# Sums of weight blocks made in DRAM by adding DMAs, in a two-layer trunk on one core

## The chip, the cores and the metric

The kernel runs on one core of a Trainium2 chip. The metric is the device time of one execution in microseconds (us); the median of three runs of the kernel before is 855.57 us, from 854.59 to 857.61. The engines of the core are TensorE (PE: matmuls, with PEld for its weight loads), VectorE (DVE), ScalarE (ACT), GpSimd (POOL) and SyncE (SP, which here only issues DMAs). Each works through its own instructions in order, and waits between engines go by semaphores.

## The reference

Two layers over 512 tokens of width 1024, each a norm, a mixer and a residual add, and a last norm. Cut to what matters:

```python
def pool_mixer(h, w_in, w_grp, scale, w_out):          # layer 0
    v, gate = jnp.split(h @ w_in, 2, axis=-1)          # 2 x 2048 columns
    p = multiscale_pool(v)                             # windows of 2, 4, 8, 16 tokens, by group of 512
    m = jnp.einsum('btgc,gcd->btgd', p, w_grp).reshape(B, T, D_INNER) * scale
    return (m * jax.nn.silu(gate)) @ w_out

def hgrn2_mixer(h, w_in, lb, norm_g, w_out):           # layer 1
    q, fz, i, gate = jnp.split(h @ w_in, 4, axis=-1)   # 4 x 2048 columns
    # forget gates f from fz, k from 1 - f; per head of 128 columns a recurrence over the tokens:
    #   S_t = diag(f_t) S_{t-1} + k_t v_t^T,   o_t = S_t^T q_t        with v = i
    # in chunks, with running products of f within a chunk
    ...
    return (o * jax.nn.silu(gate)) @ w_out

for layer in range(2):
    h = h + mixer(rms_norm(h, norm_g[layer]))          # rms_norm: h * rsqrt(mean(h*h) + eps) * g
return rms_norm(h, final_g)
```

All is in float32.

## The kernel before, in words

**Products.** A float32 product is three matmuls (`mm3`, L128): both operands are cut into a high part (a cast on ACT, L97) and a low part (a subtraction on DVE, L98). Weights come in pieces of 128 x 2 x 512 (512 KB): SP loads a piece into one of three buffers `wraw`, and `split` makes `whi` and `wlo`, six buffers each (`piece`, L100). The norm is not put into the operand: the products run on h times the norm's weights, and the norm's factor `rn`, one number for a token, is spread over the partitions by matmuls (`spread`, L192, its matmuls on L197) into `rb`, by which the results are multiplied.

**Layer 0** goes through four groups of 512 columns: values (L263), pooling on DVE (L274), gates with silu (L290; its last product is `gs` on POOL, L300), the group's product with `w_grp` (L304), and the product out (L220). The first products of group 0 don't need the factor. It is made from the squares of the tokens in the first microseconds: `ms` on DVE, then `rn_l0` on POOL (L255); the matmuls of L197 that spread it are written into the gates' first product ahead of its last two blocks (L258).

**Layer 1** goes through four groups of four heads. `prepare` (L692) makes the forget gates (`forget`, L396), their running products within a chunk by doubling steps on DVE (L698 to L702), the queries, and scales keys and queries (L713 to L723). For group 0 it also calls, by `mid`, `turn` (transposes of h) and `differences` (L433): sums and differences of the operand's four blocks (two halves of the tokens, two halves of the 1024 rows), cut in two and also stored in DRAM.

**The values of two groups at once.** `inputs2` (L464) makes the values of groups g and g + 1 for g = 0 and 2: with the operand as 2 x 2 blocks and the weights as 2 x 2 blocks of 512 x 512 (`row`: half of the inner dimension, `col`: group), seven block products do the work of eight. Four of them take a sum of weight blocks: b00 + b01, that + b11, b01 + b11, and b00 + b01 + b11 + b10. The kernel before loads the blocks and adds them on DVE (`add`, L483, traced as L485) before it cuts them (`cut`, L488), with running sums in the tile `chain`: eight adds of 128 x 1024 and 18 loads of 512 KB for a pair.

**The order.** The program is not run in the order in which it is written. A scheduler at build time goes through the instructions, engine by engine, by priority (as written, with loads and splits moved ahead by `tc.high_priority`), and puts on each engine what its own model says can go next. The result is a fixed order for each engine. No DMA is issued from POOL in the kernel before; SP issues the loads, ACT the stores.

Of the kernel before, what the change touches and what calls it, by code (L numbers as in the profile page):

```python
# [40 lines left out]
P = 128  # L41
D = 1024
T = 512
DI = 2048
# [11 lines left out]
AHEAD0 = 85  # L56
AHEAD = 300
FLOOR = 1e-26
LEVELS = (1, 2, 4, 8, 16, 32, 64)


# [5 lines left out]
def trunk(ctx: ExitStack, tc: tile.TileContext, xT, x_d, par, ident_d, causal_d, mask_d, fg_d, w0_in, w0_grp, w0_out, w1_in, w1_out, out):  # L67
# [28 lines left out]
    def split(src, hi, lo):  # L96
        nc.scalar.copy(out=hi, in_=src)  # L97
        nc.vector.tensor_tensor(out=lo, in0=src, in1=hi, op=ALU.subtract)  # L98
# [124 lines left out]
            nc.vector.tensor_tensor(out=h[n], in0=acc, in1=h[n], op=ALU.add)  # L223


    with tc.tile_pool(name="l0", bufs=1) as l0:
        xs, pieces = [], []
        wv = w0_in.rearrange("(k p) n -> p k n", p=P)
# [86 lines left out]
        zprev = None  # L315
        for g in range(NG):
            vs = values(g)
            px = pool(g, vs)
            if zprev is not None and g < NG - 1:
                project_out(load_out(w0_out, g - 1), zprev)  # L320
            gts = gates0(g)
            z = mixed(g, px, gts)
            if g == NG - 1:
                project_out(load_out(w0_out, g - 1), zprev)
            zprev = z
# [24 lines left out]
    def hgrn(ctx, general, h):  # L350
# [113 lines left out]
        def inputs2(g):  # L464

            w = w1_in.rearrange("(k p) n -> p k n", p=P)

            def block(row, col, i):
                c = 2 * DI + (g + col) * GC
                return w[:, 4 * row + 2 * i:4 * row + 2 * i + 2, c:c + GC]

            def load(*a):
                raw = wpool.tile([P, 2, GC], F32, name="wraw", tag="wraw", bufs=RAW)
                with tc.high_priority(AHEAD):
                    nc.sync.dma_start(out=raw, in_=block(*a))  # L480
                return raw

            def add(out, x, y):  # L483
                with tc.high_priority(AHEAD):
                    nc.vector.tensor_tensor(out=out, in0=x, in1=y, op=ALU.add)  # L485
                return out

            def cut(x):  # L488
                hi = wpool.tile([P, 2, GC], F32R, name="whi", tag="whi", bufs=WB)
                lo = wpool.tile([P, 2, GC], F32R, name="wlo", tag="wlo", bufs=WB)  # L490
                with tc.high_priority(AHEAD):
                    split(x, hi, lo)
                return [(hi[:, 0], lo[:, 0]), (hi[:, 1], lo[:, 1])]

            def product(accs, x, pieces):
                for b, acc in enumerate(accs):
                    t = slice(b * P, (b + 1) * P)
                    for k, ((xh, xl), (wh, wl)) in enumerate(zip(x, pieces)):
                        mm3(acc, xh[:, t], xl[:, t], wh, wl, k == 0, k == 3)

            two = lambda: [ps.tile([P, T], F32, name="mm", tag="mm", bufs=4) for _ in range(2)]
            v = l1.tile([P, TB, GC], F32, name="vn", tag="vn", bufs=1)
            v1 = [l1.tile([P, GC], F32, name="v1", tag="gs", bufs=4) for _ in range(TB)]
            chain = []
            s = (lambda i: diff[i]) if g == 0 else again

            def plus(out, acc, x):
                nc.vector.tensor_tensor(out=out, in0=acc, in1=x, op=ALU.add)

            def times(x, by, t):  # L510
                nc.scalar.activation(out=x, in_=x, func=AF.Copy, scale=by[:, t:t + 1])

            a = two()
            product(a, own[0], cut(load(0, 0, 0)) + cut(load(0, 0, 1)))
            for b in range(2):
                nc.scalar.copy(out=v[:, 2 + b], in_=a[b])
            a = two()
            product(a, own[1], cut(load(1, 0, 0)) + cut(load(1, 0, 1)))
            for b in range(2):
                plus(v[:, b], a[b], v[:, 2 + b])  # L520
                times(v[:, b], rn, b)
            pieces = []
            for i in range(2):
                x, y = load(0, 0, i), load(0, 1, i)
                chain.append(l1.tile([P, 2, GC], F32, name="chain", tag="f", bufs=2))
                pieces += cut(add(chain[i], x, y))
            c = two()
            product(c, s(0), pieces)
            s2 = s(1)
            pieces = [x for i in range(2) for x in cut(add(chain[i], chain[i], load(1, 1, i)))]  # L530
            a = two()
            product(a, s2, pieces)
            s3 = s(2)
            for b in range(2):
                plus(v1[b], a[b], v[:, 2 + b])
            pieces = []
            for i in range(2):
                x, y = load(0, 1, i), load(1, 1, i)
                pieces += cut(add(x, x, y))
            a = two()  # L540
            product(a, s3, pieces)
            s4 = s(3)
            for b in range(2):
                plus(v[:, 2 + b], a[b], v1[b])
                plus(v1[2 + b], c[b], v[:, 2 + b])
                plus(v1[b], c[b], v1[b])
                times(v1[2 + b], nrn, 2 + b)
                nc.scalar.dma_start(out=v_d[2 + b], in_=v1[2 + b])
            pieces = [x for i in range(2) for x in cut(add(chain[i], chain[i], load(1, 0, i)))]
            a = two()  # L550
            product(a, own[3], pieces)
            for b in range(2):
                plus(v[:, 2 + b], a[b], v[:, 2 + b])
                times(v[:, 2 + b], rn, 2 + b)
            a = two()
            product(a, s4, cut(load(1, 1, 0)) + cut(load(1, 1, 1)))
            for b in range(2):
                plus(v1[b], a[b], v1[b])
                times(v1[b], nrn, b)
                nc.scalar.dma_start(out=v_d[b], in_=v1[b])  # L560
            return v
# [108 lines left out]
        def factored():  # L670
# [21 lines left out]
            def prepare(g, mid=None):  # L692
                cur["first"] = firsts = [l1.tile([P, 2, TB], F32, name="first", tag="first", bufs=2) for _ in range(2)]
                es = []
                fs, ks = forget(g, store)
                for pr in range(2):
                    f, kk = fs[pr], ks[pr]
                    for hh in (1, 2, 4, 8, 16, 32):  # L698
                        x = f.rearrange("p j (b s m two h) -> p (j b) s m two h", b=TB, s=2, two=2, h=hh)
                        n = 32 // hh  # L700
                        nc.vector.tensor_tensor(out=x[:, :, 0, :, 0], in0=x[:, :, 0, :, 0], in1=x[:, :, 0, :, 1, 0:1].broadcast_to([P, 2 * TB, n, hh]), op=ALU.mult)
                        nc.vector.tensor_tensor(out=x[:, :, 1, :, 1], in0=x[:, :, 1, :, 1], in1=x[:, :, 1, :, 0, hh - 1:hh].broadcast_to([P, 2 * TB, n, hh]), op=ALU.mult)  # L702

                    en = ends[:, g * GT + 2 * pr:g * GT + 2 * pr + 2]
                    fv = f.rearrange("p j (b s c) -> p j b s c", b=TB, s=2)
                    nc.gpsimd.tensor_copy(out=en[:, :, :, 0], in_=fv[:, :, :, 0, 0])
                    nc.gpsimd.tensor_copy(out=en[:, :, :, 1], in_=fv[:, :, :, 1, 63])
                    e = l1.tile([P, 4, 2, TB], F32, name="e", tag="e", bufs=2)[:, 0]
                    nc.gpsimd.tensor_tensor(out=e, in0=firsts[pr], in1=en[:, :, :, 0], op=ALU.mult)
                    es.append(e)  # L710
                if mid:
                    mid()
                qs = queries(g)  # L713
                for pr in range(2):
                    for j in range(2):
                        r = l1.tile([P, T], F32, name="r", tag="r", bufs=2)
                        nc.gpsimd.tensor_scalar(out=r, in0=fs[pr][:, j], scalar1=FLOOR, scalar2=None, op0=ALU.max)  # L717
                        nc.vector.reciprocal(out=r, in_=r)  # L718
                        rv, fv, kv, qv = halved(r), halved(fs[pr][:, j]), halved(ks[pr][:, j]), halved(qs[pr][:, j])
                        nc.gpsimd.tensor_tensor(out=kv[:, :, 0], in0=kv[:, :, 0], in1=fv[:, :, 0], op=ALU.mult)  # L720
                        nc.gpsimd.tensor_tensor(out=kv[:, :, 1], in0=kv[:, :, 1], in1=rv[:, :, 1], op=ALU.mult)  # L721
                        nc.vector.tensor_tensor(out=qv[:, :, 0], in0=qv[:, :, 0], in1=rv[:, :, 0], op=ALU.mult)  # L722
                        nc.vector.tensor_tensor(out=qv[:, :, 1], in0=qv[:, :, 1], in1=fv[:, :, 1], op=ALU.mult)  # L723
                cur["k"], cur["q"], cur["e"] = ks, qs, es
# [242 lines left out]
```

## Time and profile before

| | |
|---|---|
| median of three runs | 855.57 us (854.59 to 857.61) |
| profiled execution | 856.04 us, span 854.2 us, mean granted clock 0.986 |
| PE busy | 818.0 us, 96% of the span |
| DVE busy | 606.8 us, 71% |
| ACT busy | 302.2 us, 35% |
| POOL busy | 153.9 us, 18% |
| DMA | 104.24 MB, mean 122 GB/s |

Layer 0 takes about the first 314 us, layer 1 the rest. "Busy" counts the instructions of an engine, not the issuing of DMAs. PEclk in the slices is the clock that TensorE was granted, in tenths of its full speed (9 is 0.9 or more); 0.5 of full speed is the lower of its two levels, 1.2 GHz against 2.4. "Idle before" an instruction is put down to what released it last.

### The profile page before, as it was taken

Reading aid. Unit: us, or ns where it says so; the run is one execution under the profiler, and the core shown is the slowest. Engines: PE = TensorE matmul, PEld = TensorE weight load, DVE = VectorE, ACT = ScalarE, POOL = GpSimd, SP = SyncE. Lnnn points to the kernel's source line nnn. Section 1 sums busy time; section 2 is a strip of 40 time slices with the busy share of each in tenths; the row PEclk is TensorE's granted clock in tenths of the full one; section 3 lists DMA queues with packets and bytes.
Section 4 is the critical chain, followed back from the end, with each engine's and each line's share of the span. In section 5 each row is a group of like instructions: output and inputs, shape, how many; then the busy total and the mean of one; then the engine's idle time right before and its main releaser. Section 6 shows DMA issues by size and latency. Waiting matters only on the chain.

```text
span 854.2 us, 10355 instructions
## 1 busy us (share of the span) xinstructions
PE 818.0 (96%) x3854; PEld 681.8 (80%) x3854; DVE 606.8 (71%) x917; ACT 302.2 (35%) x508; POOL 153.9 (18%) x198
## 2 busy tenths in 40 slices
PE   9999999999999999977899998999988999998995
PEld 8888888888888888856688887888867888887984
DVE  5687546835777464998856996569988645996764
ACT  7442223223234254433544313223135143313222
POOL 0020010001020050620022332103300021332200
PEclk9999999999999999987999999999999999999999
DMA  9532233322124353156764221223178343221202
GB/s 348 174 100 80 70 117 128 99 99 98 50 99 151 94 183 107 60 196 197 229 214 148 79 79 43 96 99 91 58 256 277 106 148 99 79 84 57 79 2 101
DMA packets 52172, 104.24 MB, mean 122 GB/s; under 512 B 3984, under 2 KB 8336, under 8 KB 52112
## 3 DMA queue, kind: packets, MB, share of 16 engines
q1 hardware_dynamic: 45056, 91.24, 32.7%
q10 hardware_dynamic: 7056, 12.25, 3.9%
q8 instruction: 32, 0.52, 0.3%
q14 instruction: 28, 0.23, 0.1%
HBM read 92.99 MB, written 10.49 MB: 121 GB/s over the span
## 4 chain that ended last, share of the span: by engine, by line
PE 78%; DVE 14%; DMA 4%; issue 2%; ACT 1%; POOLq 0%; DVEq 0%; SPq 0%; POOL 0%; ACTq 0%
PE mm L129 24%; PE mm L130 23%; PE mm L131 23%; DVE r L718 4%; DVE wlo L98 3%; DMA wraw<-in_w1i 3%; PE a L773 2%; PE a L775 1%; DVE chain L485 1%; PE a L751 1%; DVE q L722 1%; PE a L86 1%; DMA wraw<-in_w1o 1%; DVE q L723 1%; PE a L734 1%
## 5 line engine op out<-in xcount | busy, mean ns | idle before, releaser
L129 PE MATMUL mm<-xh,whi 128*128 128x512 f32 x624 | 245.0, 393 | 0.0
L130 PE MATMUL mm<-xl,whi 128*128 128x512 f32 x624 | 243.1, 390 | 0.0
L131 PE MATMUL mm<-xh,wlo 128*128 128x512 f32 x624 | 243.1, 390 | 0.0
L97 ACT CAST whi<-wraw 128x1024 fp32r<-128x1024 f32 (+1 forms) x140 | 141.6, 1025 | 206.8 <-PE mm L130 100.3
L98 DVE TENSOR_TENSOR wlo<-wraw,whi 128x1024 fp32r<-128x1024 f32 (+1 forms) x140 | 172.5, 1256 | 46.1 <-ACT whi L97 44.8
L131 PEld LDWEIGHTS mm<-xh,wlo 128*128 128x128 f32 x624 | 117.3, 188 | 24.7
L129 PEld LDWEIGHTS mm<-xh,whi 128*128 128x128 f32 x624 | 117.4, 188 | 24.3 <-DVE h L223 0.3
L130 PEld LDWEIGHTS mm<-xl,whi 128*128 128x128 f32 x624 | 117.4, 188 | 23.8
L718 DVE RECIPROCAL r<-r 128x512 f32<-128x512 f32 x16 | 53.4, 3340 | 1.0 <-POOL r L717 1.0
L130 PE MATMUL mm<-zl,whi 128*128 128x512 f32 x128 | 49.8, 389 | 0.0
L129 PE MATMUL mm<-zh,whi 128*128 128x512 f32 x128 | 49.8, 389 | 0.0
L131 PE MATMUL mm<-zh,wlo 128*128 128x512 f32 x128 | 49.8, 389 | 0.0
L130 PE MATMUL mm<-wlo,z1h 128*128 128x512 f32 x112 | 45.4, 406 | 3.1 <-DVE wlo L98 3.1
L129 PE MATMUL mm<-whi,z1h 128*128 128x512 f32 x112 | 45.8, 414 | 1.9 <-ACT whi L97 1.9
L131 PE MATMUL mm<-whi,z1l 128*128 128x512 f32 x112 | 45.2, 404 | 0.0
L223 DVE TENSOR_TENSOR h<-mm,h 128x512 f32<-128x512 f32 x32 | 21.9, 688 | 28.3 <-PE mm L131 28.0
L380 DVE TENSOR_TENSOR ht<-mm,ht 128x512 f32<-128x512 f32 x32 | 22.0, 686 | 22.3 <-PE mm L131 22.3
L300 POOL TENSOR_TENSOR gs<-gt,sg 128x512 f32<-128x512 f32 x16 | 21.9, 1374 | 87.6 <-ACT sg L298 87.6
L580 POOL TENSOR_TENSOR gs<-fz,s 128x512 f32<-128x512 f32 x16 | 21.5, 1344 | 84.1 <-ACT s L578 83.9
L721 POOL TENSOR_TENSOR kk<-kk,r 128x256 f32<-128x256 f32 x16 | 21.5, 1343 | 59.6 <-DVE r L718 59.6
L592 POOL TENSOR_TENSOR ro<-mo,mhalf 128x4 f32<-128x4 f32 x16 | 16.2, 1014 | 77.4 <-DVE mo L590 77.4
L734 PE MATMUL a<-q,kk 128*128 128x128 f32 x128 | 19.0, 290 | 10.9 <-DVE q L723 5.5
(178 smaller groups left out, 1311.2 us busy)
## 6 DMA issues: line engine op xcount, KB each, us to landing
wraw<-in_w1i SPq DMA_DIRECT2D x84, 512.0 KB, 4.2
wraw<-in_w0i SPq DMA_DIRECT2D x28, 512.0 KB, 4.3
wraw<-in_w0o SPq DMA_DIRECT2D x16, 512.0 KB, 3.8
wraw<-in_w1o SPq DMA_DIRECT2D x16, 512.0 KB, 4.4
wraw<-in_w0g SPq DMA_DIRECT2D x8, 512.0 KB, 3.7
s<-sums_fac SPq DMA_DIRECT2D x16, 256.0 KB, 5.0
h<-in_xT SPq DMA_DIRECT2D x8, 256.0 KB, 5.2
wraw<-in_w0i SPq DMA_DIRECT2D x8, 256.0 KB, 5.3
```

The lines of the kernel that those rows point to most:

```text
L97: nc.scalar.copy(out=hi, in_=src)
L98: nc.vector.tensor_tensor(out=lo, in0=src, in1=hi, op=ALU.subtract)
L129: nc.tensor.matmul(out, lh, rh, start=start, stop=False)
L130: nc.tensor.matmul(out, lh, rl, start=False, stop=False)
L131: nc.tensor.matmul(out, ll, rh, start=False, stop=stop)
L223: nc.vector.tensor_tensor(out=h[n], in0=acc, in1=h[n], op=ALU.add)
L300: nc.gpsimd.tensor_tensor(out=gs, in0=gt, in1=sg, op=ALU.mult)
L380: nc.vector.tensor_tensor(out=ht[b][:, c], in0=acc, in1=ht[b][:, c], op=ALU.add)
L580: nc.gpsimd.tensor_tensor(out=gs, in0=gt, in1=sg, op=ALU.mult)
L718: nc.vector.reciprocal(out=r, in_=r)
L721: nc.gpsimd.tensor_tensor(out=kv[:, :, 1], in0=kv[:, :, 1], in1=rv[:, :, 1], op=ALU.mult)
L734: nc.tensor.matmul(a[:, b], k[:, t], q[:, t], start=True, stop=True)
```

## The change

1. The sums of weight blocks of both pairs are made in DRAM, in four blocks `wsum[g][0..3]` of 512 x 512 for each pair, by 32 DMAs of 512 KB that POOL issues: half of them copy a block, half add a block to what is there (`accum_op`). They come in six steps, called from layer 0's loop in groups 1 to 3. POOL is the engine that issues DMAs which add.
2. `inputs2` loads each of its seven weight operands ready-made, four from `wsum`, by `piece`: 14 loads for a pair, and no add on DVE.
3. In `prepare`, `mid` is called before the running products instead of after them: this moves `turn` and `differences` of group 0.
4. The memory set aside for DMA descriptors of POOL goes from 512 to 1024.

```diff
+    wsum = {g: dram.tile([4, 4 * P, GC], F32, name=f"wsum{g}") for g in PAIRS}   # PAIRS = (0, 2)
+
+    def quarter(g, row, col):
+        c = 2 * DI + (g + col) * GC
+        return w1_in[row * 4 * P:(row + 1) * 4 * P, c:c + GC]
+
+    def weight_sums(step):
+        for g in PAIRS:
+            w5, w6, w7, w4 = (wsum[g][i] for i in range(4))
+            todo = (((w5, quarter(g, 0, 0), False), (w7, quarter(g, 0, 1), False)),
+                    ((w5, quarter(g, 0, 1), True), (w7, quarter(g, 1, 1), True)),
+                    ((w6, w5, False),), ((w6, quarter(g, 1, 1), True),),
+                    ((w4, w6, False),), ((w4, quarter(g, 1, 0), True),))[step]
+            for out_, in_, adding in todo:
+                for r in range(0, 4 * P, 2 * P):
+                    if adding:
+                        nc.gpsimd.dma_start(out=out_[r:r + 2 * P], in_=in_[r:r + 2 * P], accum_op=ALU.add)
+                    else:
+                        nc.gpsimd.dma_start(out=out_[r:r + 2 * P], in_=in_[r:r + 2 * P])
...
         for g in range(NG):
             vs = values(g)
+            if g:
+                weight_sums(2 * g - 2)
             px = pool(g, vs)
...
             gts = gates0(g)
+            if g:
+                weight_sums(2 * g - 1)
             z = mixed(g, px, gts)
...
-            def add(out, x, y):
-                with tc.high_priority(AHEAD):
-                    nc.vector.tensor_tensor(out=out, in0=x, in1=y, op=ALU.add)
...
-            pieces = []
-            for i in range(2):
-                x, y = load(0, 0, i), load(0, 1, i)
-                chain.append(l1.tile([P, 2, GC], F32, name="chain", tag="f", bufs=2))
-                pieces += cut(add(chain[i], x, y))
             c = two()
-            product(c, s(0), pieces)
+            product(c, s(0), pieces(wsum[g][0]))
             s2 = s(1)
-            pieces = [x for i in range(2) for x in cut(add(chain[i], chain[i], load(1, 1, i)))]
             a = two()
-            product(a, s2, pieces)
+            product(a, s2, pieces(wsum[g][1]))
...
                 fs, ks = forget(g, store)
+                if mid:
+                    mid()
                 for pr in range(2):
...
-                if mid:
-                    mid()
                 qs = queries(g)
...
-    nc = bacc.Bacc("TRN2", target_bir_lowering=False, num_devices=1, dynamic_dma_scratch_size=512)
+    nc = bacc.Bacc("TRN2", target_bir_lowering=False, num_devices=1, dynamic_dma_scratch_size=1024)
```

The order of the built programs shows where the scheduler puts this. Lines of the kernel after are some 20 to 30 higher: its L278 is L255 of before, L292 is L269, L323 is L300.

POOL at the start of the program, before; `v` are the first four value tiles, `rn_l` the layer's norm factor:

```order
L82 MEMSET ones 128x128
L94 MEMSET mhalf 128x8
L269 MEMSET v 128x16 x4
L255 ISA
L255 TENSOR_TENSOR rn_l_327<-ms,mhalf 128x4
L269 MEMSET v 128x16 x2
L300 TENSOR_TENSOR gs<-gt,sg 128x512 x2
```

The same place after, from the row behind the four memsets of `v`; `wsum_104` and `wsum_105` are the sums of the first and of the second pair, L246 copies and L244 adds, and the copies inside `wsum` are first those to `w6`, then those to `w4`:

```order
L246 DMA wsum_104<-in_w1i 256x512 x4
L246 DMA wsum_105<-in_w1i 256x512 x4
L244 DMA wsum_104<-in_w1i 256x512 x4
L244 DMA wsum_105<-in_w1i 256x512 x4
L246 DMA wsum_104<-wsum_104 16x8192 x2
L246 DMA wsum_105<-wsum_105 16x8192 x2
L244 DMA wsum_104<-in_w1i 256x512 x2
L244 DMA wsum_105<-in_w1i 256x512 x2
L246 DMA wsum_104<-wsum_104 16x8192 x2
L246 DMA wsum_105<-wsum_105 16x8192 x2
L278 ISA
L278 TENSOR_TENSOR rn_l_329<-ms,mhalf 128x4
```

Of the 32 DMAs 28 now stand between the first memsets and `rn_l`; the last four, which add to `w4`, follow right behind `rn_l`, ahead of the next memsets of `v` and of `gs`.

DVE in the first pair's stretch, before; `d` are the differences (L441 to L444), `q<-q,r` and `q<-q,f` the queries' scaling:

```order
L718 RECIPROCAL r<-r 128x512
L441 TENSOR_TENSOR d<-t 128x256
L443 TENSOR_TENSOR d<-t 128x256
L442 SCALAR_TENSOR_TENSOR d<-d,t 128x256
L722 TENSOR_TENSOR q<-q,r 128x4x64
L444 SCALAR_TENSOR_TENSOR d<-t,d 128x256
L723 TENSOR_TENSOR q<-q,f 128x4x64
L98 TENSOR_TENSOR z1l<-d,z1h 128x512
L485 TENSOR_TENSOR chain<-wraw 128x1024
L98 TENSOR_TENSOR s<-d,s 128x512
```

After, an earlier place in DVE's list, where the differences (L468 to L471) now stand among the running products (L701, L702):

```order
L468 TENSOR_TENSOR d<-t 128x256
L470 TENSOR_TENSOR d<-t 128x256
L469 SCALAR_TENSOR_TENSOR d<-d,t 128x256
L701 TENSOR_TENSOR f<-f 128x8x2x16
L471 SCALAR_TENSOR_TENSOR d<-t,d 128x256
L702 TENSOR_TENSOR f<-f 128x8x2x16
L99 TENSOR_TENSOR z1l<-d,z1h 128x512
L701 TENSOR_TENSOR f<-f 128x8x32
L99 TENSOR_TENSOR s<-d,s 128x512
L702 TENSOR_TENSOR f<-f 128x8x32
L446 TENSOR_TENSOR q<-mm,rb 128x512 x2
```

Two of the four rounds of differences moved in front of the queries' products, two stay behind them, and the adds into `chain` are gone.

## Rows read from the trace of the kernel before

**Rows 1.** Page: busy shares and, by slice, PE and its clock.
```profile
PE 818.0 (96%) x3854; PEld 681.8 (80%) x3854; DVE 606.8 (71%) x917; ACT 302.2 (35%) x508; POOL 153.9 (18%) x198
...
PE   9999999999999999977899998999988999998995
...
PEclk9999999999999999987999999999999999999999
```

**Rows 2.** Busy time by stretch, start of layer 0 (columns in the first line).
```profile
core 0: us, PE busy (x) PEld busy (x) DVE busy (x) ACT busy (x) POOL busy (x), PEclk, DMA share, GB/s
...
5.00:20.00 15.00, 15.00 (x64) 12.28 (x64) 10.61 (x16) 12.90 (x22) 0.00 (x0) 1.00 1.03 393
20.00:32.00 12.00, 12.00 (x55) 9.94 (x54) 6.04 (x6) 6.38 (x7) 1.01 (x1) 1.00 0.71 245
32.00:36.00 4.00, 4.00 (x23) 3.46 (x22) 2.10 (x4) 2.70 (x3) 0.00 (x0) 1.00 0.62 205
```

**Rows 3.** Busy time by stretch, both pairs' values and the low clock between.
```profile
345.00:430.00 85.00, 70.50 (x303) 56.79 (x302) 77.69 (x110) 35.10 (x48) 21.44 (x20) 0.88 0.55 179
378.00:394.00 16.00, 8.35 (x30) 6.17 (x29) 15.19 (x18) 4.03 (x8) 2.61 (x2) 0.64 0.55 193
394.00:404.00 10.00, 9.68 (x33) 7.84 (x34) 8.04 (x10) 4.43 (x6) 0.00 (x0) 0.72 0.71 219
575.00:675.00 100.00, 93.28 (x439) 76.23 (x439) 90.90 (x135) 35.14 (x44) 17.51 (x20) 1.00 0.53 169
```

**Rows 4.** Waits of PE, 345 to 430 us: total, times, longest (us).
```profile
PE a L734 <- DVE q L723: 5.5, 3, 3.5
PE mm L130 <- DVE wlo L98: 3.7, 2, 3.1
PE mm L129 <- DVE v L508: 3.4, 1, 3.4
```

**Rows 5.** Timeline of POOL, 0 to 60 us: start, duration, instruction, idle before.
```profile
0.90 0.24 POOL L269 MEMSET v<- 128x16 f32 x4
...
21.47 1.01 POOL L255 TENSOR_TENSOR rn_l<-ms,mhalf 128x4 f32<-128x4 f32 x1 [20.34 <-DVE ms L253]
40.46 0.11 POOL L269 MEMSET v<- 128x16 f32 x1 [17.98 <-DVE win L284]
...
41.80 3.27 POOL L300 TENSOR_TENSOR gs<-gt,sg 128x512 f32<-128x512 f32 x2
```

**Rows 6.** Timeline of PE, 30 to 34 us, at the spreading matmuls.
```profile
32.19 1.05 PE L197 MATMUL a<-ident,rn_l 128*128 128x128 f32 x8
33.00 0.48 PE L129 MATMUL a<-xh,whi 128*128 128x512 f32 x1
```

**Rows 7.** Line L485, the adds on DVE: duration min/median/max in ns.
```profile
L485 DVE TENSOR_TENSOR chain<-chain,wraw x8: 1206/1221/1226, 383.0 to 644.2; 128x1024 f32<-128x1024 f32 x8
L485 DVE TENSOR_TENSOR chain<-wraw x4: 1154/1208/1210, 375.1 to 623.8; 128x1024 f32<-128x1024 f32 x4
L485 DVE TENSOR_TENSOR wraw<-wraw x4: 1203/1222/1226, 398.3 to 638.8; 128x1024 f32<-128x1024 f32 x4
```

**Rows 8.** Waits of SP's DMA queue, 0 to 60 us: total, times, longest.
```profile
SPq L106 <- DVE wlo L98: 32.8, 11, 15.1
```

**Rows 9.** DMA issues: count, KB each, median us from issue to landing.
```profile
wraw<-in_w1i SPq DMA_DIRECT2D x84, 512.0 KB, 4.2
...
h<-in_xT SPq DMA_DIRECT2D x8, 256.0 KB, 5.2
wraw<-in_w0i SPq DMA_DIRECT2D x8, 256.0 KB, 5.3
xt<-in_x SPq DMA_DIRECT2D x4, 512.0 KB, 6.7
hmid<-h ACTq DMA_DIRECT2D x8, 256.0 KB, 2.2
```

**Rows 10.** Timeline of DVE, 54 to 55 us: the first reader of gs.
```profile
54.45 0.73 DVE L311 SCALAR_TENSOR_TENSOR z<-mm,pp,gs 128x512 f32<-128x512 f32 x1
```

More of the change, by code (lines that the diff above doesn't have):

```diff
@@ L58 @@
 FLOOR = 1e-26
+PAIRS = (0, 2)
 LEVELS = (1, 2, 4, 8, 16, 32, 64)
@@ L464, in inputs2, with pieces, product @@
         def inputs2(g):
[L471 to L478, printed above, removed]
-                with tc.high_priority(AHEAD):
-                    nc.sync.dma_start(out=raw, in_=block(*a))
-                return raw
-            def add(out, x, y):
-                with tc.high_priority(AHEAD):
-                    nc.vector.tensor_tensor(out=out, in0=x, in1=y, op=ALU.add)
-                return out
[L488 to L495, printed above, removed]
+            def pieces(src):
+                v = src.rearrange("(k p) n -> p k n", p=P)
+                out = []
+                for i in range(0, 4, 2):
+                    hi, lo = piece(v[:, i:i + 2])
+                    out += [(hi[:, 0], lo[:, 0]), (hi[:, 1], lo[:, 1])]
+                return out
+            def product(accs, x, w):
                 for b, acc in enumerate(accs):
                     t = slice(b * P, (b + 1) * P)
-                    for k, ((xh, xl), (wh, wl)) in enumerate(zip(x, pieces)):
+                    for k, ((xh, xl), (wh, wl)) in enumerate(zip(x, w)):
                         mm3(acc, xh[:, t], xl[:, t], wh, wl, k == 0, k == 3)
@@ L503, in inputs2 @@
             v1 = [l1.tile([P, GC], F32, name="v1", tag="gs", bufs=4) for _ in range(TB)]
-            chain = []
             s = (lambda i: diff[i]) if g == 0 else again
@@ L513, in inputs2 @@
             a = two()
-            product(a, own[0], cut(load(0, 0, 0)) + cut(load(0, 0, 1)))
+            product(a, own[0], pieces(quarter(g, 0, 0)))
             for b in range(2):
@@ L517, in inputs2 @@
             a = two()
-            product(a, own[1], cut(load(1, 0, 0)) + cut(load(1, 0, 1)))
+            product(a, own[1], pieces(quarter(g, 1, 0)))
             for b in range(2):
@@ L535, in inputs2 @@
                 plus(v1[b], a[b], v[:, 2 + b])
[L536 to L539, printed above, removed]
             a = two()
-            product(a, s3, pieces)
+            product(a, s3, pieces(wsum[g][2]))
             s4 = s(3)
@@ L548, in inputs2 @@
                 nc.scalar.dma_start(out=v_d[2 + b], in_=v1[2 + b])
-            pieces = [x for i in range(2) for x in cut(add(chain[i], chain[i], load(1, 0, i)))]
             a = two()
-            product(a, own[3], pieces)
+            product(a, own[3], pieces(wsum[g][3]))
             for b in range(2):
@@ L555, in inputs2 @@
             a = two()
-            product(a, s4, cut(load(1, 1, 0)) + cut(load(1, 1, 1)))
+            product(a, s4, pieces(quarter(g, 1, 1)))
             for b in range(2):
```

## The prediction

> **What bounds the kernel now.** I read the page's busy shares first. TensorE (PE) is busy 96% of the span [rows 1], so every microsecond in which PE stands still is close to a microsecond of the result, and work on other engines counts only where PE waits for it. The slices show where PE is not full: layer 0 is full, 9s in every slice to the first values' stretch, and there is a dip in slices 18 to 20, where the granted clock falls too [rows 1]. The table by stretches puts numbers on both. From 5 to 36 us PE is busy every microsecond at clock 1.00 [rows 2]. In the stretch of the first pair's values, 345 to 430 us, it is busy 70.5 of 85 us; the clock is 0.64 from 378 to 394 us, where PE is half idle, and still 0.72 in the ten after it, where it works again. The second pair's stretch, 575 to 675 us, has 6.7 us idle [rows 3]. So the change can win only in those two stretches, and layer 0 has no slack to pay with.
>
> Then I read the waits of PE in the first stretch: nearly all end on VectorE (DVE): q 5.5 us, wlo 3.7, v 3.4, that is 12.6 of the 14.5 idle [rows 4]; DVE is itself busy 77.7 of those 85 us [rows 3]. DVE is what limits that stretch.
>
> Last I read the start of layer 0, since the diff puts DMAs on GpSimd (POOL). POOL writes four small memsets at 0.90 us and is then idle until the layer's norm factor rn_l (L255) at 21.47, which takes 1.01 us [rows 5]. PE reaches the matmuls that spread this factor (L197) at 32.19 us, in the midst of the gates' first product, and goes straight on [rows 6]. Everything after them in layer 0 needs rb.
>
> **The change part by part.**
>
> *The adds that go.* Sixteen adds of 1.21 to 1.22 us on DVE (8, 4 and 4) [rows 7], 19.5 us, half in each stretch: 9.7 us of DVE work in each. The eight loads that go with them are a side matter: the PE waits of the first stretch name DVE, not a DMA [rows 4]. What can be won in the first stretch is at most its idle time and what the low clock took: 14.5 us, and 8.35 x 0.36 + 9.68 x 0.28 = 5.7 us of slower work [rows 3], together 20.2. DVE is nearly full there, so I take about the DVE time removed, 10 us. In the second stretch at most 6.7 us; I take 4.
>
> *The differences ahead of the running products.* Nothing is added; 16 subtractions on half rows (256 columns) and their splits stand earlier on DVE, and the running products, the reciprocals and the queries' products later. PE waits for q on DVE already [rows 4], so this can cost as well: I count it at 0, from -5 (what q's wait is now) to what is in the bound above. The two gains together: 14 us, from -5 to 27.
>
> *The sums in DRAM.* The code calls for them in groups 1 to 3 of layer 0, but the order of the built program has 28 of the 32 DMAs on POOL in front of rn_l, right behind the four memsets. 8 copies go first; each of the 8 adds waits for the copy under it, the 4 copies to w6 for the adds to w5, the 4 adds to w6 for those, and the 4 copies to w4 for these. A DMA-issuing queue stands still at a DMA whose wait isn't met: SP spent 32.8 us so in the first 60 us, behind DVE [rows 8]. So rn_l cannot start before 24 DMAs of 0.524 MB, 12.6 MB, have landed in four rounds, and PE stops at L197 until then.
>
> When is that? Beside it run the layer's first loads: 8 + 8 of 0.262 MB, 4 of x and 4 of the gates' weights of 0.524, 8.4 MB (the first 20 from the issues [rows 9], the last four from the code of load_in). From 5 to 20 us the DMA engines are full (share 1.03) at 393 GB/s [rows 2]. No DMA from DRAM to DRAM, none that adds and none issued by POOL is in the trace, so these are bounded by such rows.
> - First loads: 8.4 / 0.393 = 21.3 us.
> - 12 copies, 6.3 MB at the same rate: 16.0 us.
> - 12 adds, 6.3 MB: an add has to read its destination as well as its source. One pass would be 16.0 us, two 32.0; I take two.
> - Four handovers from landing to the next issue: 4 x 2.2, the median landing of the short writes hmid [rows 9], 8.8 us.
> - POOL begins at about 1.1 us; rn_l itself 1.0 us [rows 5].
>
> The sum is 80.2 us, against 32.2 at which PE asks for it: PE stands for 48 us. That the first loads land later beside the sums costs nothing by itself: the work in front of L197 ends at 32 us now and has until 80. The low end: no load in the way and adds in one pass, 42.9 us, a stop of 10.7. The high end: one DMA after the other, each as long as a weight load from issue to landing, 24 x 4.2 = 100.8 and 2.1, a stop of 70.7; at the 6.7 us of the xt loads, which landed among other loads, 130.7 [rows 9]. I stay at 48, near the full rate, as POOL may have several copies in flight.
>
> *Behind rn_l.* Four adds to w4 still stand in front of the memsets and of gs, which POOL reaches 8 to 10 us after L197 now [rows 5, 6]. They wait for the copies to w4, 2.1 MB: 5.3 + 2.2 = 7.5 us. The first reader of gs, z on DVE, stands 22 us behind L197 [rows 6, 10]. I count 0, up to 10 if the four go out one by one (16.8 us more).
>
> *The clock.* After a stretch with PE half idle at 0.64 the next ten microseconds ran at 0.72 [rows 3], 2.8 us lost. After a stop of 48 us I add 3, from 0 to 6.
>
> **Sum.** The profiled execution took 856.0 us with a span of 854.2; the median of the runs is 855.6, 0.5 less. 856.0 + 48 + 3 - 14 = 893.0, and on the median's footing 892.5, so 893.
>
> The Trainium skill ("DMA: Bandwidth & Descriptors", section Latency and other measured facts) has copies between HBM tensors, from the SP and ACT queues, at 214 GB/s at best; no run here shows one. By the Trainium skill's figure the copies would take 29 us and the adds 59, rn_l would come at 120 us, PE would stand for 88 and the time would be an estimated 933.
>
> **The rivals.**
> 1. *The sums go out slower, one or two at a time.* For it: each adding DMA waits for its own copy and nothing in the trace shows POOL issuing DMAs at all. Against: the DMA engines do take many transfers at once [rows 2]. A stop of 70.7, 3 for the clock, 3 behind rn_l, 14 back: 919. The figure of the Trainium skill above lies on this side.
> 2. *The sums cost only their bytes.* Adds in one pass and the gates' loads (2.1 MB, 5.3 us) behind them: rn_l at 58.9, a stop of 26.7, 2 for the clock, 18 back: 867.
> 3. *Faster: the stop is smaller than what the values' stretches give back.* The mechanism is the same, POOL in front of rn_l, with all loads out of the way: rn_l at 42.9, a stop of 10.7 and 18 back, 849. It decides at a stop of 14 us, rn_l at 46. Against: 12.6 + 8.4 MB by then would be over 450 GB/s, and the full engines gave 393 [rows 2].
> 4. *POOL does not stop:* the waits are kept by the DMA queues, and rn_l passes. Then only the gain is left, 856 - 14 = 842. Against it is SP's row [rows 8]. The Trainium skill says so too ("DMA: Bandwidth & Descriptors", section Anatomy of one DMA): DMA engines wait for no semaphore, the issuing sequencer does, before dispatch. By that rule, the trace's 32.8 us on SP agree.
>
> **How the numbers follow.** Forecast (876 to 905) 0.45; rival 1 (905 and more) 0.25; rival 2 (859 to 876) 0.20; rivals 3 and 4 together 0.10, of which 0.02 within what can be told. Faster means by over 0.3%, 2.6 us, which is about what a measurement of this kernel tells from no change. So faster 0.08, same 0.02, slower 0.90. The range leaves out rivals 3 and 4 and the far end of rival 1: 864 to 935; the likeliest case alone is 876 to 905.
>
> **What would show it.** Right: in the profile after, the first dip of PE stands in layer 0, in slices 1 to 3; PE idles in front of the spreading matmuls, released by POOL's rn_l; rn_l starts at 60 to 100 us; DMA traffic is high to there; the granted clock falls in the stop; the two values' stretches are shorter by 8 to 20 us together, with no add on DVE. The stop then shifts all that follows. Wrong: rn_l before 46 us, or PE passing L197 near 32 us, would make it faster; PE idle in layer 0 at other places (weights late, gs late) would leave the sum right for a wrong reason; a values' stretch that is no shorter would say that DVE's adds were hidden.

## The result and the profile after

The kernel after takes 933.33 us in the median of four runs (931.47 to 939.08), the kernel before 855.37 beside it: a ratio of 1.0918, with a 95% interval of 1.0866 to 1.0971. It is slower by 78 us. The forecast was 893, in a range of 864 to 935: the sign, the place and the mechanism were right, but the loss is over twice the 37 us that were forecast, and the time lies at the far end of the range.

The page of the kernel after, busy shares and the slices of PE and of its granted clock, which answers to [rows 1]:

```profile
PE 824.5 (89%) x3854; PEld 685.7 (74%) x3854; DVE 589.2 (63%) x901; ACT 301.8 (32%) x508; POOL 179.0 (19%) x230
...
PE   8600299999999999999969999899998999998995
...
PEclk9855599999999999999969999999999999999998
```

The first dip is now at the start of layer 0: in the third to the fifth slice (47 to 116 us) PE is empty or nearly so, and its clock is at half of full speed, 1.2 GHz; the second slice (23 to 47 us) is busy to six tenths. DVE's busy time fell from 606.8 to 589.2 us, by 17.6 us: the 16 adds are gone from it.

The waits of PE in the first 200 us, as in [rows 4]:

```profile
PE a L198 <- POOL rn_l L278: 66.5, 1, 66.5
```

66.5 us in one piece, released by POOL's `rn_l`. The timeline of PE there, which answers to [rows 6], from a wait for a cut of the weights that came late to the first matmuls behind the stop (start, duration, what; in brackets the idle time before it):

```profile
36.69 0.79 PE L130 MATMUL a<-xh,whi 128*128 128x512 f32 x1 [5.43 <-ACT whi L98]
...
41.95 0.63 PE L132 MATMUL a<-xh,wlo 128*128 128x512 f32 x1
42.38 0.63 PE L130 MATMUL a<-xh,whi 128*128 128x512 f32 x1
...
43.79 0.39 PE L132 MATMUL a<-xh,wlo 128*128 128x512 f32 x1
...
110.67 2.07 PE L198 MATMUL a<-ident,rn_l 128*128 128x128 f32 x8 [66.50 <-POOL rn_l L278]
```

PE comes to the spreading matmuls at 44.2 us instead of 32.2 and starts them at 110.67. After the wait of 5.43 us for the weights the matmuls stand 0.43 us apart (41.95 and 42.38) instead of 0.23: from 36.69 to 42.80 us the granted clock is 0.50, the lower level. The table by stretch, with the columns of [rows 2]:

```profile
36.00:60.00 24.00, 7.45 (x18) 5.10 (x18) 6.13 (x5) 4.82 (x5) 2.66 (x3) 0.57 0.77 186
60.00:80.00 20.00, 0.00 (x0) 0.00 (x0) 0.00 (x0) 0.00 (x0) 4.65 (x7) 0.50 0.62 101
```

To 36 us the DMA engines are full (a share of 1.02 with 395 GB/s from 5 to 20 us, 1.06 with 363 from 20 to 36), but now the first loads share this with the copies. Then, from 36 to 80 us, they are **not** full any more: a share of 0.77 and 0.62, 186 and 101 GB/s, while PE stands still from 44 us. Something else than bandwidth holds the sums. It is seen on POOL, in its timeline, which answers to [rows 5] (start, duration, what; L246 copies, L244 adds; in brackets the idle time before it):

```profile
1.42 1.98 POOL L246 DMA_DIRECT2D wsum<-in_w1i  x3 [0.27 <-issue]
...
22.71 0.96 POOL L244 DMA_DIRECT2D wsum<-in_w1i  x1 [4.11 <-issue]
...
74.92 0.89 POOL L244 DMA_DIRECT2D wsum<-in_w1i  x1 [5.09 <-issue]
...
102.74 0.89 POOL L244 DMA_DIRECT2D wsum<-in_w1i  x1 [5.22 <-issue]
...
109.54 1.08 POOL L278 TENSOR_TENSOR rn_l<-ms,mhalf 128x4 f32<-128x4 f32 x1
...
131.50 2.84 POOL L323 TENSOR_TENSOR gs<-gt,sg 128x512 f32<-128x512 f32 x2
```

Three copies go out at once and five more about every 2 us (9.29 to 18.03). But each add goes out alone, 7.5 us behind the one before it in the mean of the first eight (22.71 to 74.92, seven intervals). What POOL waits for in between is mostly not another instruction's semaphore but "issue", which means that the profile shows nothing it waited for; in the waits of POOL (first 200 us) this is by far the largest row. The 16 adds of line L244 took 5.9 us in the median from issue to landing, and no two were issued closer than 5.97: each went out about when the one before it had landed. The DMA issues, as in [rows 9], show what the copies did to the first loads:

```profile
POOL wsum L244 <- issue: 84.9, 14, 10.0
```

```profile
DMA to landing us min/median/max: 5.7/5.9/10.6
```

```profile
wraw<-in_w0i SPq DMA_DIRECT2D x8, 256.0 KB, 11.0
```

The first weights landed 11.0 us after their issue in the median, instead of 5.3.

Where the rest of the time goes is read from landmarks on the chain of work that ended last: the spreading of layer 1's factor, and the transposes of the first heads in groups 0, 1 and 2. Before, then after:

```profile
332.82 0.89 PE a L197 x8
...
458.96 0.87 PE a L604 x8
...
564.77 0.87 PE a L604 x8
...
715.15 0.87 PE a L604 x8
```

```profile
417.39 0.89 PE a L198 x8
...
538.16 0.87 PE a L602 x8
...
645.35 0.87 PE a L602 x8
...
791.47 0.87 PE a L602 x8
```

The shift of after against before is 78.5 us at layer 0's spreading (110.67 against 32.19), 84.6 at layer 1's, 79.2 in group 0 behind the first pair's values, 80.6 in group 1, 76.3 in group 2 behind the second pair's, and 76.4 at the end of the span. So: 78.5 lost by the stop, 6.1 more behind it in layer 0, 5.4 and 4.3 won back in the two values' stretches, 1.4 lost between them.

Two waits stand in what was lost behind the stop (first 200 us):

```profile
DVE gt L319 <- POOL gs L323: 7.5, 1, 7.5
PE mm L131 <- DVE pl L99: 2.0, 1, 2.0
```

DVE stood 7.5 us, to 133.16, before it could write its third gate `gt`, since POOL's first `gs` came only at 131.50, behind the four adds to `w4`. DVE's cut `pl` of the pooled values stands behind that gate in DVE's list, and PE waited 2.0 us for it, to 134.96. The clock was low twice: 0.50 from 110.67 to 114.6 us and 0.51 from 135 to 138, which is about 2.0 and 1.5 us of work. Together that is 5.5 of the 6.1 us.

In the values' stretches, the waits of PE of the kernel after from 420 to 520 us:

```profile
PE a L732 <- DVE q L720: 7.7, 3, 4.2
...
PE a L732 <- DVE q L721: 1.2, 1, 1.2
```

The waits for `wlo` and `v` of [rows 4] are gone from this stretch; the wait for q is not.

### The profile page after: what moved, and what is told of

It reads as the page before. It is cut to its first block, busy times and chain, and to the rows that moved or that the text cites. A ratio compares the mean times of both kernels' runs of the same rounds, so it can differ in the third digit from the quotient of the medians.

```text
span 930.6 us, 10388 instructions
## 1 busy us (share of the span) xinstructions
PE 824.5 (89%) x3854; PEld 685.7 (74%) x3854; DVE 589.2 (63%) x901; ACT 301.8 (32%) x508; POOL 179.0 (19%) x230
## 4 chain that ended last, share of the span: by engine, by line
PE 73%; issue 11%; DVE 8%; DMA 4%; POOL 2%; ACT 1%; POOLq 0%; SPq 0%; DVEq 0%; ACTq 0%
PE mm L131 22%; PE mm L130 22%; PE mm L132 22%; DVE r L716 3%; DVE wlo L99 2%; DMA wraw<-wsum 2%; PE a L771 2%; POOL wsum L244 1%; PE a L773 1%; PE a L749 1%; PE a L732 1%; DMA wsum<-wsum 1%; DMA wsum<-in_w1i 1%; DMA s<-sums_fac 1%; ACT whi L98 1%
## 5 line engine op out<-in xcount | busy, mean ns | idle before, releaser
L98 ACT CAST whi<-wraw 128x1024 fp32r<-128x1024 f32 (+1 forms) x152 | 154.1, 1027 | 232.7 <-PE mm L131 99.7
L99 DVE TENSOR_TENSOR wlo<-wraw,whi 128x1024 fp32r<-128x1024 f32 (+1 forms) x152 | 187.3, 1256 | 58.1 <-ACT whi L98 56.8
L198 PE MATMUL a<-ident,rn_l 128*128 128x128 f32 x8 | 2.1, 441 | 66.5 <-POOL rn_l L278 66.5
L293 DVE TENSOR_TENSOR v<-mm,rb 128x512 f32<-128x512 f32 x16 | 10.8, 686 | 73.0 <-ACT rb L204 66.8
L323 POOL TENSOR_TENSOR gs<-gt,sg 128x512 f32<-128x512 f32 x16 | 21.4, 1358 | 87.1 <-ACT sg L321 87.0
```

The lines of the kernel that those rows point to most:

```text
L293: nc.vector.tensor_tensor(out=v[:, 16:], in0=acc, in1=rb, op=ALU.mult)
L323: nc.gpsimd.tensor_tensor(out=gs, in0=gt, in1=sg, op=ALU.mult)
```

## The experiments

The first theory, A, after the profile: one add at a time leaves POOL because the memory set aside for DMA descriptors, 1024, holds one add of 512 KB but three copies; everything behind on POOL, `rn_l` first, waits for that. The rival, B: an adding DMA is slow by itself, or is held by the one that wrote the block before it.

**e1, the adds made plain copies.** It leaves out the adding.

```diff
-                        nc.gpsimd.dma_start(out=out_[r:r + 2 * P], in_=in_[r:r + 2 * P], accum_op=ALU.add)
+                        nc.gpsimd.dma_start(out=out_[r:r + 2 * P], in_=in_[r:r + 2 * P])
```

> The kernel after, with the 16 adding DMAs made plain copies of the same blocks (leaves out the adding; order of every engine as in the kernel after). Theory A, adds leave POOL one at a time because the memory for descriptors holds one add but three copies: the second 8 DMAs go out about every 2.0 us as the first 8 copies did, not every 6.1; 24 x 2 us and four handovers put rn_l at 55 to 65 us instead of 109.5, and the time at 880 to 890 us. Theory B, any DMA that has to write what an earlier one wrote is held that long, whatever it does: the pace stays near 6 us, rn_l near 105, the time near 930.

Measured: 881.63 us in one run (855.35 for the kernel before beside it). Its POOL timeline, at the same 24 DMAs (L244 are now copies too):

```profile
20.04 0.56 POOL L244 DMA_DIRECT2D wsum<-in_w1i  x1 [1.40 <-issue]
...
38.73 0.57 POOL L244 DMA_DIRECT2D wsum<-in_w1i  x1 [1.92 <-issue]
...
62.65 1.06 POOL L278 TENSOR_TENSOR rn_l<-ms,mhalf 128x4 f32<-128x4 f32 x1
```

The second eight go out every 2.7 us (18.7 us for seven), not every 7.5 as in the kernel after (52.2 for seven), and `rn_l` comes at 62.65 us. The block under each of them was written by the first eight just as before. So it is the adding that costs, not the chain of writes: B's second form falls. From 20 to 39 us the DMA engines are full here, at 413 GB/s in all. Behind that, from 39 to 63 us, most of the traffic is copies from DRAM to DRAM; POOL's queue (packets, MB, share of the engines' time):

```profile
q0 software_dynamic: 1113, 6.87, 74.8%
```

That is 286 GB/s for these copies, beside 2.27 MB of weight loads.

**e2, twice the memory for descriptors.**

```diff
-    nc = bacc.Bacc("TRN2", target_bir_lowering=False, num_devices=1, dynamic_dma_scratch_size=1024)
+    nc = bacc.Bacc("TRN2", target_bir_lowering=False, num_devices=1, dynamic_dma_scratch_size=2048)
...
```

The room comes from two small tiles of layer 1 (`e` at its used size, one buffer for `m` in place of two), and a branch that does not run is left out. That costs nothing that can be seen: from layer 1's spreading to the end this run takes 510.3 us, the kernel after 513.2.

> The kernel after, with the memory for DMA descriptors of POOL at 2048 instead of 1024 (room for it from two small tiles, and the fallback branch for other inputs, which does not run here, is left out). Theory A: three adds fit instead of one, so they go out in runs of two or three and the pace falls from 6.1 us an add to 2 to 4 us; rn_l at 65 to 90 us, time 885 to 912. Theory B, an add is slow in the DMA engines or waits for a round trip of its own: pace still 6 us, rn_l at 105 to 110, time 925 to 935.

Measured: 897.65 us in one run, against 855.35. The same place on POOL, and the table of stretches:

```profile
1.40 4.17 POOL L246 DMA_DIRECT2D wsum<-in_w1i  x7 [0.26 <-issue]
...
12.37 0.96 POOL L244 DMA_DIRECT2D wsum<-in_w1i  x1 [3.23 <-issue]
...
45.66 0.89 POOL L244 DMA_DIRECT2D wsum<-in_w1i  x1 [4.40 <-issue]
...
59.27 0.91 POOL L244 DMA_DIRECT2D wsum<-in_w1i  x1 [8.91 <-DMA wsum<-wsum]
...
61.94 0.86 POOL L244 DMA_DIRECT2D wsum<-in_w1i  x1 [0.38 <-DMA wsum<-wsum]
69.16 0.89 POOL L244 DMA_DIRECT2D wsum<-in_w1i  x1 [6.36 <-issue]
...
81.46 1.07 POOL L278 TENSOR_TENSOR rn_l<-ms,mhalf 128x4 f32<-128x4 f32 x1
```

```profile
12.00:46.00 34.00, 21.24 (x79) 13.49 (x77) 8.66 (x12) 11.74 (x19) 6.59 (x8) 0.95 1.08 305
46.00:82.00 36.00, 9.88 (x18) 4.99 (x18) 6.30 (x6) 5.57 (x7) 8.63 (x14) 0.50 1.07 301
```

Seven copies go out at once instead of three, and where several adds are ready, three go within 2.7 us (59.27 to 61.94); the fourth waits until 69.16. In the kernel after no add followed another in less than 5.97 us. The first eight adds take 33.3 us for seven intervals, 4.8 each, instead of 7.5, and `rn_l` comes at 81.46 instead of 109.54. An add takes 12.9 us to land in the median, against 5.9 in the kernel after, so at a pace of 4.8 two or three are under way. The DMA engines are now full in both stretches (1.08 and 1.07), but at 305 and 301 GB/s, where the copies of e1 had 413. So both theories hold a part: with 1024 the adds go one by one, and more memory lets them overlap; and the full engines move less with adds than with copies.

**e3, each add in two halves.**

```diff
-                for r in range(0, 4 * P, 2 * P):
+                n = P if adding else 2 * P
+                for r in range(0, 4 * P, n):
...
```

> The kernel after, with each add cut into two DMAs of 128 rows (256 KB). The order changes with it: only the adds to w5 and w7 (16 half adds) and six to eight copies stand in front of rn_l, the rest behind it, mixed with gs and the memsets. Theory A (space for descriptors): two or three half adds fit at once, a half add every 2 to 3 us, so rn_l at 60 to 75 us and the time at 885 to 905. Theory B with a fixed round trip for each adding DMA: a half add costs nearly what an add does, 5 to 6 us, rn_l at 105 to 120, time 925 to 945. Theory B with a rate of the DMA engines: 3 us for a half add, rn_l at 70 to 80.

Measured: 892.22 us in one run. Its POOL timeline, first and last of the 16 half adds in front of the factor:

```profile
20.05 0.89 POOL L245 DMA_DIRECT2D wsum<-in_w1i  x1 [1.28 <-issue]
...
58.02 0.82 POOL L245 DMA_DIRECT2D wsum<-in_w1i  x1 [1.62 <-issue]
...
60.62 1.37 POOL L279 TENSOR_TENSOR rn_l<-ms,mhalf 128x4 f32<-128x4 f32 x1
```

16 half adds from 20.05 to 58.02, 2.5 us each, 5.1 for the two halves of what took 7.5. A half add takes 6.8 us to land in the median, at a pace of 2.5: with the same memory as in the kernel after, DMAs of half the size overlap, as A has it. So a fixed round trip of 5 to 6 us before the next one may go (B) is ruled out, and B as a rate of the engines had `rn_l` at 70 to 80 us, where it came at 60.62. The factor is earlier here than in e2, but the time is not much less: sixteen half adds still stand behind it, among the `gs`, and PE waits 8.8 us for cuts of the pooled values.

**e4, the factor taken off POOL.**

```diff
-            nc.gpsimd.tensor_tensor(out=rn, in0=ms, in1=mhalf[:, :TB], op=ALU.pow)
+            nc.scalar.activation(out=ms, in_=ms, func=AF.Sqrt)
+            nc.vector.reciprocal(out=rn, in_=ms)
```

> The kernel after, with layer 0's norm factor made by a square root on ACT and a reciprocal on DVE instead of on POOL; the 32 DMAs stand in front of the memsets and gs as before. Theory A, POOL's whole list is late and not one instruction: PE passes the spreading matmuls at 42 to 48 us, and stops 20 to 40 us later, since z needs gs, which POOL reaches behind the last add at about 131; the time falls only by the work that PE does ahead, 12 to 30 us, to 903 to 921. Rival: only rn_l was needed early, gs has slack enough: the time falls by the stop, to about 866.

Measured: 926.93 us in one run. PE passes the spreading matmuls and stands still a little later; the waits of PE (first 200 us) and of DVE (first 140 us):

```profile
PE mm L130 <- DVE gt L320: 65.0, 1, 65.0
```

```profile
DVE gt L320 <- POOL gs L324: 66.9, 2, 66.4
```

The instruction next in POOL's list takes the place of the first. DVE has two buffers for `gt`, and POOL's `gs` frees them; `gs` now stands behind all 32 DMAs. The expected 903 to 921 was missed by 6 us: I had let PE run on to the first `z`, but it stops at the third gate, at 69.0 us.

**e5, the sums left out.** The four products load one block each in place of a sum.

```diff
-            if g:
-                weight_sums(2 * g - 2)
...
-            product(c, s(0), pieces(wsum[g][0]))
+            product(c, s(0), pieces(quarter(g, 0, 1)))
...
```

> The kernel after without the 32 DMAs; the four products with a sum of blocks load a single block of in_w1i instead (leaves out the sums of weight blocks; the order on PE, DVE and ACT is that of the kernel after). Theory A, all of the loss is POOL standing still in layer 0: PE passes L198 at 32 us and the time is that of before less what the values' stretches gave back in the kernel after, 8 us: 845 to 849, ratio to before about 0.990. Rival, the changed order or the loads from DRAM sums cost too: above 852.

Measured: 848.89 us in the median of six runs, 857.11 for the kernel before in 17, ratio 0.9907 (0.9888 to 0.9926): 8.0 us won. (The ratios are as recorded for the sets of runs; they differ a little from the quotients of the two medians.) So all that the kernel after loses comes with the 32 DMAs, by their place on POOL or by their traffic; e9 tells these apart. Nothing is lost in the new order on PE, DVE and ACT, which is the same here.

**e6, the same with the differences in their old place.**

```diff
                 fs, ks = forget(g, store)
-                if mid:
-                    mid()
...
+                if mid:
+                    mid()
                 qs = queries(g)
```

> As e5, but with the differences behind the running products again, where the kernel before has them (leaves out the sums of weight blocks). It shows what taking the adds off DVE is worth alone. If the adds carry the gain: 846 to 851. If the earlier differences carry it: 853 to 857.

Measured: 848.28 us in the median of six, ratio 0.992 (0.9893 to 0.9946). **e7, the differences alone** is e6's move made in the kernel before, the other way round:

```diff
                 fs, ks = forget(g, store)
+                if mid:
+                    mid()
...
-                if mid:
-                    mid()
                 qs = queries(g)
```

> The kernel before with only the differences moved ahead of the running products. If the adds carry the gain, 853 to 858, as before. If the earlier differences carry it, 848 to 851; if they cost, over 859.

Measured: 856.23 us in the median of twelve, ratio 0.9996 (0.9982 to 1.0009). The adds carry the gain, 0.8%, together with the eight loads that go with them, which no run takes away alone; the moved differences are worth nothing that can be told, though the two intervals of e5 and e6 leave room for one or two microseconds.

**e8, the sums held back.** If the place on POOL is the fault, another place must win. In the kernel after, the late place in the source did not hold the copies back, so here each of the eight sum blocks gets a small store from a group's last `gs` ahead of its copies, which then have to wait for that group:

```diff
+    def weight_sums(group, late):
+        plan = (((0, 0), (0, 2)), ((0, 1), (2, 0)), ((0, 3), (2, 2)), ((2, 1), (2, 3)))[group]
...
+                nc.scalar.dma_start(out=w[i][r:r + 16, 0:32], in_=late[0:16, 0:32])
...
             gts = gates0(g)
+            weight_sums(g, gts[3])
```

> The sums of the kernel after, but each of the eight sum blocks is held back: a small ACT store of part of a group's last gs into the block goes ahead of its copies, so that two blocks stand on POOL behind the last gs of each group of layer 0, and none in front of rn_l. Theory A: POOL has some 33 us there in which nobody waits for it, and two blocks take about 2 x (2 + 2 + 2 x 6) = 32 us, so PE does not stop: 845 to 850, faster than before. Rival, a POOL that stands for an add holds the window memsets or gs and PE behind them: 855 to 880.

Measured: 890.98 us in the median of five, ratio 1.0404 (1.0382 to 1.0427): slower than before. The rival was right. The waits of PE and of DVE, 60 to 345 us, POOL behind a group's adds, and ACT behind that:

```profile
PE mm L130 <- ACT whi L98: 26.5, 3, 11.8
PE mm L132 <- DVE wlo L99: 6.5, 3, 2.6
```

```profile
DVE win L304 <- POOL v L291: 28.6, 2, 14.7
```

```profile
87.80 0.90 POOL L245 DMA_DIRECT2D wsum<-in_w1i  x1 [5.21 <-issue]
...
88.40 0.45 POOL L291 MEMSET v<- 128x16 f32 x1
```

```profile
90.50 0.62 ACT L98 CAST ph<-p 128x512 fp32r<-128x512 f32 x1 [19.52 <-DVE p L308]
```

The factor passed in time, but the memsets of the next group's value and window tiles, 0.1 to 0.5 us each, stood behind the adds (the four at 67.17 to 87.80), and DVE's pooling behind the memsets. ACT's cast of the pooled values waits for DVE, ACT's casts of the weights stand behind it in ACT's list, and PE waits for these and for DVE's cuts: 33.0 us.

**e9, those memsets on DVE.**

```diff
-                nc.gpsimd.memset(v[:, 0:16], 0.0)
+                nc.vector.memset(v[:, 0:16], 0.0)
...
-                        nc.gpsimd.memset(nxt[:, 0:16], 0.0)
+                        nc.vector.memset(nxt[:, 0:16], 0.0)
```

> e8 with the memsets of the value and window tiles on DVE instead of POOL, so that only the products gs stand on POOL between one group's adds and the next group's. Theory A, what e8 lost was these memsets held behind the adds, and gs has room: PE does not stop in layer 0, 846 to 852, ratio to before 0.988 to 0.996. Rival, the adds' DMA traffic or gs itself hold PE up: 860 to 880.

Measured: 848.97 us in the median of six, 856.81 for the kernel before in 17, ratio 0.9921 (0.9900 to 0.9942). This computes all that the reference does, and beats both kernels. PE's slices, busy time to 345 us, and POOL around the first group's adds:

```profile
PE   9999999999999999986999998999979999998995
```

```profile
0.00:345.00 345.00, 344.01 (x1542) 286.06 (x1543) 218.33 (x346) 131.91 (x174) 60.59 (x70) 1.00 0.58 173
```

```profile
89.64 0.90 POOL L245 DMA_DIRECT2D wsum<-in_w1i  x1 [7.12 <-issue]
112.98 1.29 POOL L322 TENSOR_TENSOR gs<-gt,sg 128x512 f32<-128x512 f32 x1 [22.44 <-ACT sg L320]
```

PE is busy 344.0 of 345 us, as with no sums at all (344.0 in e5), with 16.8 MB of sums beside it: spread over the groups, their traffic costs nothing. POOL is done with the group's adds at 90.5 us and is next asked for something at 113.

**e10, the half adds of e3 in e9.**

```diff
-            for r in range(0, 4 * P, 2 * P):
-                nc.gpsimd.dma_start(out=w[i][r:r + 2 * P], in_=more[r:r + 2 * P], accum_op=ALU.add)
+            for r in range(0, 4 * P, P):
+                nc.gpsimd.dma_start(out=w[i][r:r + P], in_=more[r:r + P], accum_op=ALU.add)
```

> e9 with each add cut into two DMAs of 128 rows. If e9 is free of stops, nothing is left to win: the same as e9 within 0.3%. If in e9 an add still blocks something at the end of a group, this is faster than e9 by the 1.2 us an add that e3's pace (2.4 us a half add against 6.1 an add) saves, up to 5 us in all.

Measured: 848.72 us, ratio 0.9909 (0.9891 to 0.9928), the same as e9: where nobody waits for POOL, the pace of the adds is worth nothing.

**e11, the memsets moved in the kernel before**, by e9's diff.

> The kernel before with only those memsets on DVE, to tell what they are worth by themselves. PE does not wait for POOL in layer 0, so nothing: 853 to 858, ratio 0.997 to 1.003. If this alone is faster by 5 us or more, e9's gain is not the sums'.

Measured: 856.74 us, ratio 1.0004 (0.9993 to 1.0016): nothing, so e9's gain is that of the adds and their loads taken away.

## Why the prediction was wrong

*The mechanism* was right at each step that was read from the built order: 28 DMAs in front of `rn_l`, PE stopped at the spreading matmuls and released by `rn_l`, high DMA traffic at first, the clock at its lower level in the stop, all that follows shifted. Only the time of `rn_l`, 109.5 us, lies outside the 60 to 100 us that were named as a sign. e5 and e9 show that the place on POOL, at the start and in front of what others wait for, is the whole loss: the same sums, later on POOL and with the short memsets off it, cost nothing.

*The step that failed* is the term "12 adds, 6.3 MB: ... two [passes] 32.0", with the sentence "I stay at 48, near the full rate, as POOL may have several copies in flight". Copies it has; adds it has not: they went one by one, 7.5 us apart. The two passes were not far off: from 57 to 75 us, with nothing but adds under way, the engines were busy 54.5% of 18 us for 1.57 MB, 6.2 us for a MB, where e1's copies took 74.8% of 24 us for 6.87 MB, 2.6 us for a MB. An add cost them 2.4 times a copy, so even by their rate the 12 adds take 39 us and not 32; the larger part of the miss is that the engines stood empty between one add and the next. From the first add to the last one in front of `rn_l` 80 us pass, against 32 and two handovers in the sum. `rn_l` came at 109.5 us instead of 79, and the stop, counted as the shift at L197, was 78.5 us instead of 48: 30.5 of the some 40 us by which the forecast was short. The rest is 3 us more lost behind `rn_l` and 6 us less gained. One add at a time is the prediction's own first rival, "one or two at a time", with a stop of 70.7 us and a chance of 0.25. A hint at it stood in the diff, which I passed over: the memory for descriptors was doubled, to 1024, so it could be a limit. e2 is a check on the term: with room for three adds `rn_l` comes at 81.5 us, and the time is 897.65, where the forecast had 80.2 less the factor's own 1.0, and 893. It checks the sum and not its parts: the full engines moved 301 to 305 GB/s there and not 393, so that the two agree so closely is in part luck.

*The estimate from the Trainium skill's 214 GB/s* ("DMA: Bandwidth & Descriptors", section Latency and other measured facts) gave 933, which is the time that was measured, but not for that reason. It had the DMA engines slow at copies from DRAM to DRAM and `rn_l` at 120 us. But in the kernel after the engines were not full from 36 to 80 us, and POOL's copies in e1 moved 286 GB/s from 39 to 63 us, more than the figure, beside other loads. That figure is for the SP and ACT queues, and no run here has such copies from those. The agreement in the time is luck. The Trainium skill's rule that the issuing sequencer waits and not the DMA engines (same page, section Anatomy of one DMA) agrees with the trace: POOL stood 4.8 us at an add for the copy under it to land, and 3.8 us at a copy for the add to the block that it reads.

*Rival 4*, a POOL that goes on, is refuted: `rn_l` came at 109.5 us, and PE stood 66.5. *Rivals 2 and 3* needed `rn_l` at 59 and 43 us; even with all adds made copies it came at 62.65.

*The first loads beside the copies* were said to cost nothing by themselves. They made PE 12.0 us late at L197 (44.2), which is inside the stop and so cost nothing here, as the prediction argued; in e1, with less of a stop behind it, PE waits 15.4 us for the weights' cuts and only 7.1 for `rn_l`.

*Behind `rn_l`* I had 0, and *for the clock* 3; together 6.1 us were lost: 2.0 in PE's wait for a cut of the pooled values, 3.5 by the low clock, 0.6 not settled. `gs` came 20.8 us after the spreading matmuls, just inside the 22 us that were read from before for `z`. But `z` was not the first to need it: DVE's third gate needs the buffer that `gs` frees, as e4 shows too, and PE's 2.0 us come from there.

*The gain* was taken as 14 us and was 8.0 (e5, 6.3 to 9.6 by the interval; 8.3 by the landmarks of the kernel after). I had given the first stretch about the DVE time removed, 10 us, and the second 4. They gave 5.4 and 4.3, with 1.4 lost between: PE's wait for q, 5.5 us before, is 8.9 after, in the two rows of it. The moved differences have a part in that: in e6, where they stand behind again, PE waits 2.6 us for q, but 9.2 for results of ACT (`z1h` 4.4, `vn` 4.8), and the time is the same. That the differences would cost nothing was right (e7).

## What to carry to other kernels

An engine's list is one queue: a DMA put on it for a purpose nobody is in a hurry for stands in front of whatever the scheduler put behind it, down to a memset of a few tenths of a microsecond. So read the order of the built program for the engine that gets new waits, give late work a dependency that holds it back rather than a late line in the source, and move what others wait for off that engine.

Where transfers queue by number and not by bytes, a cost from bytes and rate is the low end only: look for what limits how many are under way, above all when the change itself alters that limit.

## What the runs showed of the hardware

An adding DMA of 512 KB from DRAM to DRAM: with 1024 of memory for descriptors, in the kernel after, no two issued closer than 5.97 us, and 5.9 us from issue to landing in the median; with 2048 three within 2.7 us, and 12.9 us to landing. Half the size overlaps at 1024 as well (2.5 us apart, 6.8 to landing). Three copies of 512 KB go out at once with 1024, seven with 2048. An add kept the DMA engines busy 6.2 us for a MB, a copy 2.6 (57 to 75 us of the kernel after, 39 to 63 us of e1). With several adds under way the DMA engines were full at 301 to 305 GB/s, with copies in their place at 381 to 413 (e1, 39 to 63 and 20 to 39 us). Copies from DRAM to DRAM on POOL's queue moved 286 GB/s (e1, 39 to 63 us). An add kept POOL busy for 0.9 us and a copy for 0.57, so most of the 7.5 us between two adds is standing and not work of POOL.

Behind an idle stretch of 5.4 us PE's matmuls stood 0.43 us apart, to 42.8 us, and 0.23 after it; the granted clock was 0.50 and then 0.96. In the idling from 60 to 110 us it was 0.50; it stayed at 0.50 for the first 3.9 us of work behind that, and was 1.00 from 114.6 to 122 us. Behind an idle stretch of 2.0 us, at 135 us, it was 0.51 for 3 us.
